# Attention in a hybrid encoder layer: scores and transposes take three PSUM banks in turn, the sums of two units alternate between two banks of their own

## The chip, the cores and the metric

The kernel runs on one core of a Trainium2 chip (trn2). The metric is device microseconds of one execution, lower is better. Engines are named as in the profile: PE is TensorE's matmul row and PEld its weight loads, DVE is VectorE, ACT is ScalarE, POOL is GpSimd, SP is SyncE, which issues most of the DMAs.

## The reference, cut to what matters

One encoder layer over two sequences of 1024 and 2048 tokens, each with 16 meta tokens ahead: an input projection, two branches (neighbourhood attention and mLSTM), a gated merge and an output projection. The change touches the attention branch alone:

```python
s_win = jnp.einsum('bcqhd,bwckhd->bhcqwk', q_blk, k_blk) * scale      # scores of a window
s_win = jnp.where(valid, s_win + bias, NEG)
s_met = jnp.einsum('bcqhd,bmhd->bhcqm', q_blk, km) * scale            # scores of the meta keys
p = jax.nn.softmax(jnp.concatenate([s_met, s_win], axis=-1), axis=-1)
out = einsum('bhcqm,bmhd->bcqhd', p_met, vm) + einsum('bhcqwk,bwckhd->bcqhd', p_win, v_blk)
```

## The kernel before

The kernel interleaves two streams of work on PE by hand: a "dense" one (projections, merge, output projection: the lines L218 to L220, L787 to L789, L988 to L990, L1953 to L1955) and a "sparse" one (mLSTM and attention). `run` (L2124) draws pieces of the dense stream between the steps of the sparse one, by cost numbers in microseconds that stand in the code. PE's order is therefore the order of the code. The order on DVE, ACT and the queues is chosen by a scheduler that simulates the program's timeline when it is built, so it can shift when a wait changes.

Attention is done per sequence, in two stages: `na(0, ...)` for the short one and `na(1, ...)` for the long one. A *unit* is one head, eight grid rows and one of four column blocks: 128 queries against 288 to 512 keys. The first stage has 64 units, the second 128. Unit u passes through these steps, which `na` (L1104) pipelines over four units, with dense work at each `yield`:

- step 1 of turn u: **scores** S(u), `na_scores` (L1230). Two matmuls (L1241, L1242) write a PSUM bank; then DVE adds the bias in place and takes the row's extremum (L1245).
- step 2 of turn u: **exponential** E(u), `na_exp` (L1251). ACT reads the bank and writes `prb` in SBUF (L1256). In the same step DVE scales unit u-1 (L1265, L1266).
- step 3 of turn u+2: **transposes** T(u), `na_turn` (L1268). Three or four transposes of `prb` (L1273) into a bank; ACT copies them to `pts` as the high part (L1275).
- step 4 of turn u+2: **low part** of the transposes, `na_low` (L1278). DVE reads the bank again (L1280).
- step 4 of turn u+3: **sums** O(u), `na_out` (L1282). Three or four matmuls (L1288) of the values with `pts`. Two units, an even and the following odd one, share a bank: half of 512 columns each.
- turn u+5 for an even u: the pair's sums are copied by ACT (`na_copy`, L1295) and added by two DVE instructions (`na_add`, L1302), which frees the bank.

PSUM has eight banks, given out by name (`psum`, L212) from `BANKS` (L41): three `pj` for the dense work, two `tr`, one `sc`, two `sm`.

```python
BANKS = dict(pj=3, tr=2, sc=1, sm=2)
```

A request for a name with several banks gets the one that was released longest ago, and the first matmul into it waits for whoever last read or wrote it. Before the change the scores of even units take `sc` and those of odd units `sm`; transposes take `tr`; the sums of a pair take `sm`. In the built program the scores of an odd unit u and the pair of sums that is opened in the same turn (units u-3 and u-2) stand one after the other in the same bank of `sm`, and the next odd turn uses the other one. So the first sum matmul of a pair, in step 4 of turn u, waits for E(u), which is issued in step 2 of that turn.

Of the kernel before, what the change touches and what calls it, by code (L numbers as in the profile page):

```python
# [3 lines left out]

# [1 line left out]

# [12 lines left out]
P = 128  # L19
# [56 lines left out]
def _row_types(R):  # L76

    out = []
    for t in range(R // 8):
        if t == 0:  # L80
            out.append((0, 0, 11))
        elif t == R // 8 - 1:
            out.append((2, R - 12, 12))
        else:
            out.append((1, 8 * t - 4, 15))
    return out
# [52 lines left out]
class K:  # L139
# [3 lines left out]
    def __init__(self, tc, ins, outs):  # L143
        self.tc, self.nc = tc, tc.nc
        self.xs = []
        self.i, self.o = ins, outs
        self.wreq, self.wraw, self.wrdy, self.wout = deque(), deque(), deque(), 0
        self.wseen, self.wkept, self.xkept = set(), {}, {}
        self.rwait = {}
        self.xput, self.turn, self.last, self.turns = deque(), 0, None, False  # L150
        self.marks, self.loose = {}, True
        self.need = False
        self.hold, self.early = deque(), True
        self.sides, self.qd, self.TD = [], {}, {}
# [949 lines left out]
    def na(self, s, rts):  # L1104

        tc, nc, i = self.tc, self.nc, self.i
        rows = _row_types(SEQLEN[s] // 64)
        with tc.tile_pool(name=f"na{s}{rts[0]}", bufs=1, side="right", reuse_waits="tile") as np_:
            self.qB = [np_.tile([P, 4, P], F32R, name=f"qB{j}") for j in range(2)]
            self.kx = [np_.tile([P, 16, 64], F32R, name=f"kx{j}") for j in range(2)]  # L1110
            self.gts = [np_.tile([P, 17, 48], F32, name=f"gt{j}") for j in range(2)]
            for q in self.qB:
                nc.gpsimd.dma_start(q[64:128], i["onehot"].rearrange("a (b c) -> a b c", b=4))
            for g in self.gts:
                nc.gpsimd.memset(g[:, 0, :], 0.0)
                nc.gpsimd.memset(g[:, 16, :], 0.0)
            heads = [(rt, pr, hh) for rt in rts for pr in range(4) for hh in range(2)]
            n = len(heads)
            prep = self.na_prep(np_, s, rows, heads, 0)
            self.na_bias(rows, heads, 0)  # L1120
            for k in range(6):
                next(prep, None)
                for _ in range(2 if k else 17 - 5 * s):
                    yield A_N[s]
            cur, nxt = self.head, None
            units = [(j, cb) for j in range(n) for cb in range(4)]
            ready = {}
            n_ = len(units)
            pairs = {}
            for u in range(n_ + 4):  # L1130
                if u >= 5 and u % 2:
                    self.na_copy(ready[u - 5], pairs[u - 5])
                    if u > n_:
                        self.na_add(ready[u - 5], pairs.pop(u - 5), s)
                if u < n_:
                    j, cb = units[u]
                    if cb == 0:
                        cur = self.head
                        prep = self.na_prep(np_, s, rows, heads, j + 1) if j + 1 < n else iter(())
                        next(prep, None)  # L1140
                    ready[u] = [cur, heads[j], cb, None, None, self.gts[j % 2], None]
                    self.na_scores(np_, ready[u], rows)
                    if j + 1 < n and cb == 0:
                        self.na_bias(rows, heads, j + 1)
                yield A_N[s]
                if u < n_:
                    self.na_exp(np_, ready[u])
                if 1 <= u <= n_:
                    self.na_scale(np_, ready[u - 1])
                if 5 <= u <= n_ and u % 2:  # L1150
                    self.na_add(ready[u - 5], pairs.pop(u - 5), s)
                if u < n_ and cb:
                    next(prep, None)
                if u == n_ + 3:
                    break
                yield A_N[s]
                if 2 <= u <= n_ + 1:
                    self.na_turn(np_, ready[u - 2])
                    if u < n_ and cb >= 2:
                        next(prep, None)  # L1160
                yield A_N[s]
                if 2 <= u <= n_ + 1:
                    self.na_low(ready[u - 2])
                if u >= 3:
                    if u % 2:
                        pairs[u - 3] = self.psum("sm", [P, 512])
                    self.na_out(ready[u - 3], pairs[(u - 3) // 2 * 2])
                yield A_N[s]
# [61 lines left out]
    def na_scores(self, np_, unit, rows):  # L1230
        nc = self.nc
        (stk, qb, kd, vt, yg, zt), (rt, pr, hh), cb = unit[:3]
        gt, c0 = unit[5], OFFC[cb] + 1
        typ, _, nr = rows[rt]
        ns = nr + 1
        kc, nb, g0 = KC0[cb], NKB[cb], (5, 1, 0)[typ]
        w, N = 8 * nb, 8 * nb * ns
        self.turns = not self.turns
        sc = self.psum("sc" if self.turns else "sm", [P, 512])
        so = sc[:, :N].rearrange("p (a b) -> p a b", b=w)  # L1240
        nc.tensor.matmul(so, stk[:, cb, :], kd[:, :ns, kc:kc + w], start=True, stop=False)  # L1241
        nc.tensor.matmul(so, qb[:, cb, :], self.kx[hh][:, :ns, kc:kc + w], start=False, stop=True)  # L1242
        pr_ = np_.tile([P, 512], F32, name="prb", bufs=3)
        mx = np_.tile([P, 1], F32, name="mx", bufs=4)
        nc.vector.tensor_tensor_reduce(  # L1245
            out=so, in0=so, in1=gt[:, g0:g0 + ns, c0:c0 + w],
            op0=ALU.add, op1=ALU.min, scale=-1.0, scalar=3.0e38, accum_out=mx)
        unit[3] = (pr_, mx, nb, 8 * ns)
        unit[6] = sc
# [18 lines left out]
    def na_turn(self, np_, unit):  # L1268
        nc = self.nc
        pr_, _, nb, ks = unit[3]  # L1270
        pt = self.psum("tr", [P, 4, P])
        for ch in range(nb):
            nc.tensor.transpose(pt[:ks, ch, :], pr_[:, ch * ks:(ch + 1) * ks], self.ident)  # L1273
        pts = np_.tile([P, 4, 2, P], F32R, name="pts", bufs=2)
        nc.scalar.activation(pts[:ks, :nb, 0, :], pt[:ks, :nb], AF.Copy)  # L1275
        unit[4], unit[6] = pts, pt
# [930 lines left out]
```

## Time and profile before

| | |
|---|---|
| time, median of 3 | 2664.87 us (2664.18 to 2667.11) |
| profiled execution, its own time | 2665.67 us |
| its span, first to last instruction | 2663.9 us |
| mean granted TensorE clock | 0.997 |
| first attention stage | about 815 to 1175 us of the span |
| second attention stage | about 1928 to 2556 us |
| last dense work behind it | 2556 to 2664 us |

A row of a view of groups has the source line, the engine, the operation, the tiles (written, then read), how many, the busy time, the mean of one, and the idle time of the engine just before them with what ended it. A row of the view of waits reads: engine, tile and line that waited, what it waited for; total, times, longest. A row of the timeline reads: start, duration, engine, line, operation, and in brackets the idle time of its engine before it with what ended it. Matmuls are pipelined and their ends are modelled: a PE row's duration is longer than the distance to the next row's start, so a short stall can hide under the row ahead of it.

### The profile page before, as it was taken

Reading aid. Unit: us, or ns where it says so; the run is one execution under the profiler, and the core shown is the slowest. Engines: PE = TensorE matmul, PEld = TensorE weight load, DVE = VectorE, ACT = ScalarE, POOL = GpSimd, SP = SyncE. Lnnn points to the kernel's source line nnn. Section 1 sums busy time; section 2 is a strip of 40 time slices with the busy share of each in tenths; the row PEclk is TensorE's granted clock in tenths of the full one; section 3 lists DMA queues with packets and bytes.
Section 4 is the critical chain, followed back from the end, with each engine's and each line's share of the span. In section 5 each row is a group of like instructions: output and inputs, shape, how many; then the busy total and the mean of one; then the engine's idle time right before and its main releaser. Section 6 shows DMA issues by size and latency. Waiting matters only on the chain.

```text
span 2663.9 us, 46683 instructions
## 1 busy us (share of the span) xinstructions
PE 2635.1 (99%) x15928; PEld 2328.5 (87%) x15928; DVE 1915.0 (72%) x5070; ACT 1423.7 (53%) x3292; POOL 196.3 (7%) x418
## 2 busy tenths in 40 slices
PE   9999999999999999999999999999999999999998
PEld 7898897899988999878888888878889898989888
DVE  5655678788776877546676776857478889797854
ACT  5423555555445554546665676656366655656521
POOL 0111131011301124000000000000000000000000
PEclk9999999999999999999999999999999999999999
DMA  9899988799866999978889998899899899898965
GB/s 371 328 332 337 332 302 303 279 339 344 313 218 242 352 324 309 317 230 268 261 269 342 370 295 260 282 348 324 275 323 321 283 306 286 284 306 266 326 244 206
DMA packets 393517, 800.47 MB, mean 300 GB/s; under 512 B 50528, under 2 KB 173360, under 8 KB 389440
## 3 DMA queue, kind: packets, MB, share of 16 engines
q1 hardware_dynamic: 361728, 697.24, 77.9%
q0 software_dynamic: 31552, 100.25, 10.2%
q8 instruction: 126, 2.06, 0.3%
q14 instruction: 111, 0.91, 0.1%
HBM read 543.72 MB, written 253.60 MB: 299 GB/s over the span
## 4 chain that ended last, share of the span: by engine, by line
PE 91%; DMA 4%; DVE 3%; ACT 1%; issue 1%; SPq 0%; DVEq 0%; ACTq 0%
PE pj L218 10%; PE pj L220 10%; PE pj L219 10%; PE pj L988 8%; PE pj L990 8%; PE pj L989 8%; PE pj L787 5%; PE pj L789 5%; PE pj L788 5%; PE pj L1954 3%; PE pj L1953 3%; PE pj L1955 3%; PE sm L1288 3%; PE tr L1273 2%; PE sm L220 1%; PE sm L219 1%
## 5 line engine op out<-in xcount | busy, mean ns | idle before, releaser
L218 PE MATMUL pj<-xh,whl 128*128 128x512 f32 (+1 forms) x960 | 369.7, 385 | 3.1 <-ACT xh L445 2.5
L220 PE MATMUL pj<-xh,whl 128*128 128x512 f32 (+1 forms) x960 | 361.0, 376 | 0.0
L219 PE MATMUL pj<-xl,whl 128*128 128x512 f32 (+1 forms) x960 | 360.3, 375 | 0.2 <-DVE xl L446 0.2
L787 PE MATMUL pj<-whl,xh 128*128 128x256 f32 (+1 forms) x1152 | 329.0, 286 | 0.0
L789 PE MATMUL pj<-whl,xl 128*128 128x256 f32 (+1 forms) x1152 | 325.3, 282 | 0.0
L788 PE MATMUL pj<-whl,xh 128*128 128x256 f32 (+1 forms) x1152 | 324.9, 282 | 0.0
L1953 PE MATMUL pj<-whl,mh 128*128 128x256 f32 x768 | 218.3, 284 | 1.1 <-DMA whl<-w 1.1
L787 PEld LDWEIGHTS pj<-whl,xh 128*128 128x128 f32 x1152 | 217.1, 188 | 0.4
L788 PEld LDWEIGHTS pj<-whl,xh 128*128 128x128 f32 x1152 | 217.0, 188 | 0.2
L789 PEld LDWEIGHTS pj<-whl,xl 128*128 128x128 f32 x1152 | 217.0, 188 | 0.0
L1954 PE MATMUL pj<-whl,mh 128*128 128x256 f32 x768 | 216.3, 282 | 0.0
L1955 PE MATMUL pj<-whl,mlo 128*128 128x256 f32 x768 | 215.5, 281 | 0.0
L218 PEld LDWEIGHTS pj<-xh,whl 128*128 128x128 f32 x960 | 181.2, 189 | 35.3 <-ACT xh L445 3.4
L220 PEld LDWEIGHTS pj<-xh,whl 128*128 128x128 f32 x960 | 181.2, 189 | 35.0
L219 PEld LDWEIGHTS pj<-xl,whl 128*128 128x128 f32 x960 | 181.8, 189 | 30.4 <-issue 1.0
L988 PE MATMUL pj<-xh,whl 128*128 128x512 f32 x512 | 206.7, 404 | 1.3 <-ACT pj L1005 1.1
L990 PE MATMUL pj<-xh,whl 128*128 128x512 f32 x512 | 202.0, 395 | 0.0
L989 PE MATMUL pj<-xl,whl 128*128 128x512 f32 x512 | 201.1, 393 | 0.0
L1280 DVE TENSOR_TENSOR pts<-tr,pts 96x384 fp32r<-96x384 f32 (+2 forms) x192 | 118.6, 618 | 63.8 <-ACT pts L1275 62.4
L1275 ACT ACTIVATE pts<-tr 96x384 fp32r<-96x384 f32 (+2 forms) x192 | 103.5, 539 | 101.7 <-PE tr L1273 101.1
L218 PE MATMUL pj<-yh,whl 128*128 128x512 f32 x384 | 154.1, 401 | 0.0
L219 PE MATMUL pj<-yl,whl 128*128 128x512 f32 x384 | 151.5, 395 | 0.7 <-DVE yl L1855 0.7
(380 smaller groups left out, 6824.9 us busy)
## 6 DMA issues: line engine op xcount, KB each, us to landing
whl<-w SPq DMA_DIRECT2D x131, 1024.0 KB
whl<-q SPq DMA_DIRECT2D x112, 512.0 KB
w<-whl SPq DMA_DIRECT2D x36, 1024.0 KB
wraw<-wu SPq DMA_DIRECT2D x48, 512.0 KB
gt<-st SPq DMA_DIRECT2D x96, 256.0 KB
tg<-gt SPq DMA_DIRECT2D x96, 256.0 KB
q<-po POOLq DMA_DIRECT2D x26, 512.0 KB, 7.3
xt<-xt SPq DMA_DIRECT2D x24, 512.0 KB
```

The source lines that it names most:

```text
L218: mm(out, ah, bh, start=start, stop=False)
L219: mm(out, ah, bl, start=False, stop=False)
L220: mm(out, al, bh, start=False, stop=stop)
L787: nc.tensor.matmul(o, xh, wh, start=k == 0, stop=False)
L788: nc.tensor.matmul(o, xh, wl, start=False, stop=False)
L789: nc.tensor.matmul(o, xl, wh, start=False, stop=k == KT - 1)
L988: mm(bank, w[:, 0, k], xh[:, k], start=fresh and k == 0, stop=False, skip_group_check=True)
L989: mm(bank, w[:, 0, k], xl[:, k], start=False, stop=False, skip_group_check=True)
L990: mm(bank, w[:, 1, k], xh[:, k], start=False, stop=k == 3, skip_group_check=True)
L1953: nc.tensor.matmul(o, mh[:, k, xs], wh, start=clear > 0 and k == 0, stop=False)
L1954: nc.tensor.matmul(o, mh[:, k, xs], wl, start=False, stop=False)
L1955: nc.tensor.matmul(o, ml[:, k, xs], wh, start=False, stop=clear < 2 and k == KT - 1)
```

## The change

It changes which bank each product is written to and nothing else: the same instructions on every engine, and PE's in the same order. A cycle over the names `sc`, `tr`, `tr` is made at the start of a stage; each request of `na_scores` and of `na_turn` takes its next name. Scores and transposes alternate on PE from the third unit on (S(u), T(u-2), S(u+1), T(u-1), ...), so each of the three banks is used again by the third request behind. The sums of the pairs are then the only users of `sm` in the stage and alternate between its two banks.

```diff
@@ na
+            self.banks = cycle(("sc", "tr", "tr"))
             heads = [(rt, pr, hh) for rt in rts for pr in range(4) for hh in range(2)]
@@ na_scores
-        self.turns = not self.turns
-        sc = self.psum("sc" if self.turns else "sm", [P, 512])
+        sc = self.psum(next(self.banks), [P, 512])
@@ na_turn
-        pt = self.psum("tr", [P, 4, P])
+        pt = self.psum(next(self.banks), [P, 512]).rearrange("p (a b) -> p a b", a=4)
```

The field `turns` and its start value in the constructor go, and `cycle` is imported.

PE in the second attention stage, transposes T(103) and the sums O(102) behind them, which open a pair in the turn of S(105); the names in brackets are the engines whose semaphores a row waits for. Before:

```order
L220 MATMUL pj<-yh,whl 128x512
L1273 MATMUL tr<-ident,prb 128x128 [waits DVE_49,PE_49]
L1273 MATMUL tr<-ident,prb 128x128 x2
L1288 MATMUL sm<-pts,vt 128x256 [waits Activation_49]
L1288 MATMUL sm<-pts,vt 128x256 x3
L218 MATMUL pj<-yh,whl 128x512 [waits DMAHW2_49]
```

And now:

```order
L220 MATMUL pj<-yh,whl 128x512
L1273 MATMUL sc<-ident,prb 128x128 [waits DVE_49,Activation_49]
L1273 MATMUL sc<-ident,prb 128x128 x2
L1288 MATMUL sm<-pts,vt 128x256 [waits DVE_49]
L1288 MATMUL sm<-pts,vt 128x256 x3
L218 MATMUL pj<-yh,whl 128x512 [waits DMAHW2_49]
```

The order is the same. The sums' wait for ACT is gone and one for DVE stands there (the low part of their own unit); the transposes, which waited for DVE and for PE's own earlier matmuls, now wait for ACT.

The first attention stage has the same order on all engines. In the second one the scheduler places some 70 of DVE's instructions and some 35 of ACT's a few rows earlier or later, and nine DMA issues of SP. DVE at 2148 to 2151 us of the profiled span, where the scaling of unit 110 (L1266, which T(110) needs) stands; L1226 splits the values of a head, L1918 and L1922 are the merge's. Before:

```order
L1265 RECIPROCAL sm<-sm 128x1 [waits Activation_49]
L1922 TENSOR_TENSOR mlo<-tg,mh 128x512 [waits Activation_49]
L1302 TENSOR_TENSOR yg<-sm,yg 64x2x8x16 [waits Activation_49]
L1266 TENSOR_SCALAR prb<-prb,sm 128x512 [waits DVE_49]
L1226 TENSOR_TENSOR vt<-vr,vt 128x8x64 [waits DMAHW6_49,DMAHW5_49,Activation_49]
L1918 SCALAR_TENSOR_TENSOR tg<-tg,pj 128x512 [waits DMAHW7_49,PE_49]
```

And now (the lines between 1117 and 1239 count one higher, so L1227 is L1226 of before):

```order
L1265 RECIPROCAL sm<-sm 128x1 [waits Activation_49]
L1302 TENSOR_TENSOR yg<-sm,yg 64x2x8x16 [waits Activation_49]
L1227 TENSOR_TENSOR vt<-vr,vt 128x8x64 [waits DMAHW6_49,DMAHW5_49,Activation_49]
L1918 SCALAR_TENSOR_TENSOR tg<-tg,pj 128x512 [waits DMAHW7_49,PE_49]
L1922 TENSOR_TENSOR mlo<-tg,mh 128x512 [waits Activation_49]
L1266 TENSOR_SCALAR prb<-prb,sm 128x512 [waits DVE_49]
```

The scaling of unit 110 now stands behind L1226 and L1918, which it stood ahead of.

More of the change, by code (lines that the diff above doesn't have):

```diff
@@ L2 @@
 from contextlib import ExitStack, contextmanager
-from itertools import chain
+from itertools import chain, cycle
 import numpy as np
@@ L149, in __init__ @@
         self.rwait = {}
-        self.xput, self.turn, self.last, self.turns = deque(), 0, None, False
+        self.xput, self.turn, self.last = deque(), 0, None
         self.marks, self.loose = {}, True
```

## The prediction

> **What bounds the kernel now.** I read the page's busy times and its chain of waits first, then the busy time by stage, then the waits of PE and PEld on the line of the sums, and last the timeline at single stalls. The page, on engines and on the chain that ended last:
>
> ```profile
> PE 2635.1 (99%) x15928; PEld 2328.5 (87%) x15928; DVE 1915.0 (72%) x5070; ACT 1423.7 (53%) x3292; POOL 196.3 (7%) x418
> ...
> PE 91%; DMA 4%; DVE 3%; ACT 1%; issue 1%; SPq 0%; DVEq 0%; ACTq 0%
> ```
>
> PE sets the end: 99% of the span, 91% of the chain. As PE's instructions and their order stay, only time in which PE stands still can be won, plus time that new stops would cost. By stretch (start:end, length, then busy time and count of PE, PEld, DVE, ACT, POOL, then granted clock, DMA share, GB/s), the second attention stage, the dense work behind it, and two pieces of the stage:
>
> ```profile
> 1928.00:2556.00 628.00, 625.52 (x4102) 567.35 (x4101) 526.89 (x1241) 372.23 (x855) 2.05 (x4) 1.00 0.92 296
> 2556.00:2664.00 108.00, 98.70 (x649) 89.87 (x647) 53.30 (x135) 15.62 (x51) 0.00 (x0) 0.98 0.65 235
> 2110.00:2124.00 14.00, 12.69 (x65) 10.37 (x64) 13.25 (x31) 5.36 (x12) 0.00 (x0) 1.00 0.99 348
> 2350.00:2386.00 36.00, 35.11 (x177) 28.76 (x176) 35.33 (x76) 19.05 (x39) 1.02 (x2) 1.00 0.99 315
> ```
>
> The stage's PE is shown idle for 628.00 - 625.52 = 2.5 us only, while DVE has 101 us to spare over the stage, but none in the two pieces (13.25 of 14 us, 35.33 of 36). What PE and its weight loads wait for at the sums (engine, line, releaser: total, times, longest; then the view of that line, with its second releaser), and the sums in the first stage's groups:
>
> ```profile
> PE sm L1288 <- ACT prb L1256: 2.2, 4, 1.3
> ...
> PEld sm L1288 <- ACT prb L1256: 5.5, 10, 1.5
> ...
>   ACT sqj L1959: 0.3, 1
> ...
> L1288 PE MATMUL sm<-pts,vt 96*128 96x256 f32 (+1 forms) x221 | 37.1, 284 | 0.0
> ```
>
> So the sums wait for an exponential in the same bank, PE by 2.2 us in four places, PEld by 5.5 + 0.3 = 5.8 us in eleven. In the first stage the line has no idle time: nothing is to be won there. The second stage opens 64 pairs so, and only eleven show a stop.
>
> **What is removed, and its size.** The two readings differ because a PE row's modelled end covers a short stop, and a load after a 512-wide matmul shows idle time even where PE does not stop. One place calibrates that:
>
> ```profile
> 2012.21 0.40 PE L220 MATMUL pj<-yh,whl 128*128 128x512 f32 x1
> 2012.44 0.50 PE L1288 MATMUL sm<-pts,vt 96*128 96x256 f32 x2
> ...
> 2012.44 0.41 PEld L1288 LDWEIGHTS sm<-pts,vt 96*128 96x128 f32 x3 [0.28 <-ACT prb L1256]
> ```
>
> Starts of PE are 0.23 us apart, the pace of a 512-wide matmul, so PE lost nothing, though the load shows 0.28 us. After a 512-wide matmul the load's reading is thus about 0.27 too high. The largest stop, and two more of the same kind, show both cases:
>
> ```profile
> 2117.90 0.40 PE L220 MATMUL pj<-yh,whl 128*128 128x512 f32 x1
> 2118.14 0.49 PE L1273 MATMUL tr<-ident,prb 128*128 128x128 f32 x3
> 2118.72 0.49 ACT L1275 ACTIVATE pts<-tr 128x384 fp32r<-128x384 f32 x1 [3.26 <-PE tr L1273]
> 2119.11 0.68 ACT L1256 ACTIVATE prb<-sm,mx 128x512 f32<-128x512 f32 x1
> 2119.93 0.38 PE L1288 MATMUL sm<-pts,vt 128*128 128x256 f32 x1 [1.31 <-ACT prb L1256]
> 2119.93 0.19 PEld L1288 LDWEIGHTS sm<-pts,vt 128*128 128x128 f32 x1 [1.55 <-ACT prb L1256]
> ...
> 2364.97 0.40 PE L220 MATMUL pj<-yh,whl 128*128 128x512 f32 x1
> 2365.64 0.50 PE L1288 MATMUL sm<-pts,vt 128*128 128x256 f32 x2 [0.26 <-ACT prb L1256]
> 2365.63 0.41 PEld L1288 LDWEIGHTS sm<-pts,vt 128*128 128x128 f32 x3 [0.70 <-ACT prb L1256]
> ...
> 2374.79 0.49 PE L1273 MATMUL tr<-ident,prb 128*128 128x128 f32 x3
> 2375.74 0.75 PE L1288 MATMUL sm<-pts,vt 128*128 128x256 f32 x4 [0.46 <-ACT prb L1256]
> ...
> 2385.59 0.42 PEld L1288 LDWEIGHTS sm<-pts,vt 128*128 128x128 f32 x3 [0.40 <-ACT prb L1256]
> ```
>
> At 2365.64 the true loss is 2365.64 - 2364.97 - 0.23 = 0.44, which is the load's 0.70 less 0.26. At 2119.93 three transposes stand ahead; they start 2118.14 and take about 0.25 us of PE, so the loss is 1.54, which is the load's 1.55 without correction. Five of the eleven loads follow a 512-wide matmul (2012.44, 2108.99, 2267.82, 2365.64, 2501.87). **Removed: 5.8 - 5 x 0.27 = 4.5 us**, between 2.2 (PE's reading) and 5.8 (PEld's). The exponential that the sums waited for was itself queued behind the copy of the transposes on ACT (2118.72 before 2119.11), so the old wait fell where DVE, and with it the row's extremum, ran late.
>
> A page speaks to the choice: the Trainium skill, Perfetto Trace Analysis, in Identifying the Most-Contended Engine, calls matmul busy time a bad measure, since matmuls are pipelined, and weight loads' busy time a good one. By that rule the sum would use 5.8, not 4.5. The row at 2012.44 here shows the load's reading to be too high as well, so the rule is followed by half.
>
> **What is added: three kinds of waits.** Scores and transposes now take a bank whose last user is the low part (L1280, DVE) or the exponential (L1256, ACT) of the third request behind; a pair of sums takes the bank that the pair two back left to L1302. Going through all requests of both stages with the times of before, the tightest of each kind are these: transposes after an exponential, scores after a low part, sums after an addition.
>
> ```profile
> 2135.96 0.58 ACT L1256 ACTIVATE prb<-sc,mx 128x384 f32<-128x384 f32 x1
> 2138.46 0.49 PE L1273 MATMUL tr<-ident,prb 128*128 128x128 f32 x3
> ...
> 2417.88 0.56 DVE L1280 TENSOR_TENSOR pts<-tr,pts 104x384 fp32r<-104x384 f32 x1
> 2420.87 0.31 PE L1241 MATMUL sm<-kd,stk 128*128 128x312 f32 x1
> ...
> 2504.30 0.40 DVE L1302 TENSOR_TENSOR yg<-sm,yg 64x256 f32<-64x256 f32 x1
> 2511.18 0.60 PE L1288 MATMUL sm<-pts,vt 104*128 104x256 f32 x3
> ```
>
> The margins are 2138.46 - 2136.54 = 1.92 us, 2420.87 - 2418.44 = 2.43 us, and 2511.18 - 2504.70 = 6.48 us. Most requests have more than twice the first. With the times of before none of the new waits stops PE: **0**, and up to the price in the third rival below if DVE or ACT slip by more than 1.9 us against PE. Behind a stopped transpose would queue all of PE's dense work, then DVE's merge that reads `pj`. The transposes' wait for PE's own matmuls goes; it cost nothing: L220 to the transposes is 2118.14 - 2117.90 = 0.24, the dense pace.
>
> **What comes back.** PE 4.5 us earlier meets the same DVE. The sums must still wait for the low part of their own unit, now their only wait. Its tightest place, right behind the full stretch:
>
> ```profile
> 2399.12 0.56 DVE L1280 TENSOR_TENSOR pts<-tr,pts 128x384 fp32r<-128x384 f32 x1
> 2400.30 0.48 PE L1288 MATMUL sm<-pts,vt 128*128 128x256 f32 x2
> ```
>
> The margin is 2400.30 - 2399.68 = 0.62 us. From 2365 to 2386 PE wins 0.44 + 0.70 + 0.40 = 1.54 us, and DVE, which is full there, wins nothing. If the low part keeps its time, 1.54 - 0.62 = 0.92 us is lost again; if DVE uses what PE hands it earlier, 0. I take **0.5**.
>
> The scheduler's new order has one place where a wait of PE loses margin, the scaling of unit 110, now behind L1226 and L1918:
>
> ```profile
> 2149.07 0.47 DVE L1266 TENSOR_SCALAR prb<-prb,sm 128x512 f32<-128x512 f32 x1
> 2149.46 0.67 DVE L1226 TENSOR_TENSOR vt<-vr,vt 128x512 fp32r<-128x512 f32 x1
> 2150.06 0.67 DVE L1918 SCALAR_TENSOR_TENSOR tg<-tg,pj 128x512 f32<-128x512 f32 x1
> ...
> 2153.45 0.60 PE L1273 MATMUL tr<-ident,prb 128*128 128x128 f32 x4
> ```
>
> It moves by about 0.6 + 0.6 = 1.2 us (distances of the starts), of a margin of 2153.45 - 2149.54 = 3.9 us, of which PE's earlier arrival takes 1.54 + 0.35 (the stops at 2119.93 and 2149.84) = 1.9. 0.8 us are left: **0**, at worst 0.6 if the merge's L1922 stands between as well. The other moved rows of DVE and ACT have neighbours of 0.4 to 0.7 us and margins of several: 0. The nine moved DMA issues on SP load weights and merge rows; what PE lost to late weights is
>
> ```profile
> PE pj L1953 <- DMA whl<-w: 1.1, 1, 1.1
> ...
> PE pj L218 <- DMA whl<-w: 0.5, 1, 0.5
> ```
>
> so the cover, weights loaded ahead of PE, holds nearly everywhere. Moved by a place they cost 0; if the cover fails once, another stop of 0.5 to 1.1.
>
> **Sum.** -4.5 + 0 + 0.5 + 0 = -4.0 us. The profiled execution took 2665.67 (span 2663.9), which gives 2661.7 (span 2659.9). It stands 0.8 above the median of the runs, 2664.87, so the median to expect is **2660.9**; with the bounds of the terms 2658.5 (5.8 and a little from a quicker DVE) to 2663 (2.2 and nothing but small losses).
>
> **Rivals.**
>
> *First: nothing gained.* DVE is full in 2110 to 2124 and 2350 to 2386, and most of the 4.5 us lies there (1.54 + 1.54). A PE that does not wait at the sums waits a few us later at the next thing DVE owes it, the low part of the sums' own unit or the scaling ahead of the transposes. For it: the two shares, and the 0.62 margin. Against it: that margin is the least one in the stage, most others exceed 2 us, more than any single gain, and DVE has 101 us to spare over the stage in which it recovers. 4.5 - 0.5 remains in my forecast; here all but about 1 us comes back: 2664.
>
> *Second: more.* The load's idle time is right and nothing comes back: 2664.87 - 5.8 = 2659.1. For it: the weight loads run ahead and a delayed one may cost more than the distance of starts shows. Against it: the calibration at 2012.44, and at 2501.87, where the load shows 0.29 and PE's starts are 0.25 apart.
>
> *Third: slower, by the three banks.* Before, a score took its bank four units or so behind and transposes had two banks of their own; now any low part or exponential that comes 1.9 us later than today stops PE at scores or transposes. It decides where DVE is full: 14 + 36 = 50 us, at 628 / 128 = 4.9 us a unit some 10 units, each with two requests. A stop of the size of those on the sums' line (5.5 / 10 = 0.55 us) at each of the 20 would cost 11 us: 2664.9 - 4.5 + 11 = 2671.4. Against it: not one of the margins is under 1.9 us in these very stretches, and PE arrives at most 1.5 us earlier there.
>
> *Fourth: slower, by the clock.* The stage's granted clock is 1.00, in the last 108 us 0.98. Were the stage to run at 0.98, 2% of 628 = 12.6 us less the 4 would give 2673.5. Against it: the clock is 1.00 with today's stops, and fewer follow. The Trainium skill, TensorE: Matmul & The Clock Gate, in A second HAM failure mode: psum-queue depth-cycling, tells of a kernel whose PE idled shortly between groups as it cycled PSUM banks and lost clock by it; the row of 1928 to 2556 does not bear that out here.
>
> That the change does not do what it says is excluded by the order: the wait for ACT is gone from the sums' row.
>
> **Chances.** Forecast 57%, nothing gained 18%, more 13%, three banks 8%, clock 4%. A measurement of this kernel tells about 0.2% from no change, that is 5.3 us: under 2659.5 is faster, over 2670.2 slower. Faster: the 13% and a quarter of the forecast's own range (2658.5 to 2663), together 27%. Slower: 12% less a part of the third rival that stops only a few times, 10%. Same: 63%. The range runs from 2657.5 to 2667, which holds the forecast, the first rival and the second and leaves out the last two and tails.
>
> **What would show it.** Right: the row of L1288 waiting for `prb` is gone from PE and PEld; PE's idle time in the stage falls by about 2 of the 2.5 us; the gaps at 2119.93, 2365.64, 2375.74 and 2385.59 close; the span is about 2660; a new wait of the sums for `pts` of L1280 near 2395, up to 0.9. Wrong: waits of PE at L1241 or L1273 for L1280, L1256 or L1266 of a microsecond in sum; or a new wait for weights; or a granted clock under 1.00 in the stage.

## The result, and the profile after

The changed kernel took 2661.70 us (median of 20 runs, 2659.54 to 2665.48) beside 2666.91 us for the kernel before in the same comparison. One of the 20 runs of the kernel before, at 3676.39 us, lies far outside the others (2662.91 to 2669.82) and is left out of the ratio. The ratio is 0.9984 with a 95% interval of 0.9977 to 0.9990: faster by 2.7 to 6.1 us. That is about the 0.2% (5.3 us) below which the prediction calls a kernel the same, so the class is "same", though the interval over all runs is clear of zero. The profiled execution took 2659.54 us, its span 2657.6.

The page after, on the same lines as before (engines, then the chain that ended last):

```profile
span 2657.6 us, 46668 instructions
...
PE 2630.8 (99%) x15928; PEld 2326.8 (88%) x15928; DVE 1911.1 (72%) x5070; ACT 1420.7 (53%) x3292; POOL 195.7 (7%) x418
...
PE 94%; DMA 3%; DVE 2%; ACT 1%; issue 0%; SPq 0%; DVEq 0%; ACTq 0%
```

PE's share of the chain rises from 91% to 94%. By stretch, the second attention stage and the two pieces where DVE is full:

```profile
1928.00:2556.00 628.00, 628.00 (x4149) 572.89 (x4148) 525.10 (x1242) 370.33 (x856) 2.04 (x4) 1.00 0.94 297
...
2110.00:2124.00 14.00, 14.00 (x73) 11.66 (x72) 13.81 (x30) 7.88 (x17) 0.00 (x0) 1.00 1.01 374
2350.00:2386.00 36.00, 36.00 (x189) 30.33 (x188) 35.46 (x78) 20.59 (x43) 1.02 (x2) 1.00 1.01 319
```

PE shows no idle time at all in the stage (628.00 of 628.00, before 625.52), though DVE is as full in the two pieces as before. The granted clock stays 1.00.

A total over the span mixes the change with stretches that it does not touch: the time from the last sums of the first stage to the first scores of the second differs between the profiles of this study, from 740.4 to 744.1 us. So I measure **each attention stage by itself**, from its first scores matmul to its last sums matmul. For the second stage, here are the first scores and the group of all sums, before and then after (the group's row has the least, median and most duration in ns, then the first and the last start in us):

```profile
1920.28 0.30 PE L1241 MATMUL sc<-kd,stk 128*128 128x288 f32 x1
...
L1288 PE MATMUL sm<-pts,vt x672: 277/282/386, 836.7 to 2554.4; 96*128 96x256 f32 x56, 104*128 104x256 f32 x56, 128*128 128x256 f32 x56
```

```profile
1919.18 0.30 PE L1241 MATMUL sc<-kd,stk 128*128 128x288 f32 x1
...
L1288 PE MATMUL sm<-pts,vt x672: 277/282/368, 838.0 to 2548.2; 96*128 96x256 f32 x56, 104*128 104x256 f32 x56, 128*128 128x256 f32 x56
```

With the starts in hundredths: 2554.39 - 1920.28 = 634.11 us before, 2548.18 - 1919.18 = 629.00 after. The second stage is **5.1 us shorter**. The first stage takes 356.86 and 356.85. The rest of the profile's 6.1 us, 1.0, lies outside both.

Where the 5.1 us went is seen by setting PE's rows of the two traces side by side, instruction by instruction. The distance between them grows within the stage only at the first sums of pairs, by 0.1 us or more at each of twelve places that stopped before (2012.44, 2108.99, 2119.93, 2149.84, 2247.38, 2267.82, 2365.64, 2375.74, 2385.59, 2424.66, 2472.66, 2501.87). The largest one, before and after:

```profile
2117.90 0.40 PE L220 MATMUL pj<-yh,whl 128*128 128x512 f32 x1
2118.14 0.49 PE L1273 MATMUL tr<-ident,prb 128*128 128x128 f32 x3
2119.93 0.74 PE L1288 MATMUL sm<-pts,vt 128*128 128x256 f32 x4 [1.31 <-ACT prb L1256]
2120.51 0.40 PE L218 MATMUL pj<-yh,whl 128*128 128x512 f32 x1
```

```profile
2116.62 0.49 PE L1273 MATMUL sc<-ident,prb 128*128 128x128 f32 x3
2116.86 0.72 PE L1288 MATMUL sm<-pts,vt 128*128 128x256 f32 x4
2117.42 0.39 PE L218 MATMUL pj<-yh,whl 128*128 128x512 f32 x1
```

From the transposes to the matmul behind the sums it was 2.37 us, now 0.80: 1.57 us won, as the same work now runs at PE's own pace.

### The profile page after: what moved, and what is told of

Read it like the earlier page. It is cut to its first block, busy times and chain, and to the rows that moved or that the text cites. A ratio compares the mean times of both kernels' runs of the same rounds, so it can differ in the third digit from the quotient of the medians.

```text
span 2657.6 us, 46668 instructions
## 1 busy us (share of the span) xinstructions
PE 2630.8 (99%) x15928; PEld 2326.8 (88%) x15928; DVE 1911.1 (72%) x5070; ACT 1420.7 (53%) x3292; POOL 195.7 (7%) x418
## 4 chain that ended last, share of the span: by engine, by line
PE 94%; DMA 3%; DVE 2%; ACT 1%; issue 0%; SPq 0%; DVEq 0%; ACTq 0%
PE pj L218 10%; PE pj L220 10%; PE pj L219 10%; PE pj L988 8%; PE pj L990 7%; PE pj L989 7%; PE pj L787 5%; PE pj L789 5%; PE pj L788 5%; PE pj L1954 3%; PE pj L1953 3%; PE pj L1955 3%; PE sm L1288 3%; PE tr L1273 2%; PE sc L1273 1%; PE tr L1241 1%
## 5 line engine op out<-in xcount | busy, mean ns | idle before, releaser
L218 PE MATMUL pj<-xh,whl 128*128 128x512 f32 (+1 forms) x960 | 369.5, 385 | 3.8 <-ACT xh L445 2.0
L220 PE MATMUL pj<-xh,whl 128*128 128x512 f32 (+1 forms) x960 | 360.9, 376 | 0.0
L218 PEld LDWEIGHTS pj<-xh,whl 128*128 128x128 f32 x960 | 180.9, 188 | 36.2 <-ACT xh L445 2.8
L220 PEld LDWEIGHTS pj<-xh,whl 128*128 128x128 f32 x960 | 181.2, 189 | 35.0
L218 PE MATMUL pj<-yh,whl 128*128 128x512 f32 x384 | 154.1, 401 | 0.0
L220 PE MATMUL pj<-yh,whl 128*128 128x512 f32 x384 | 152.1, 396 | 0.0
L1953 PEld LDWEIGHTS pj<-whl,mh 128*128 128x128 f32 x768 | 144.7, 188 | 2.0 <-DMA whl<-w 1.2
```

The costliest lines, as they stand in the source:

```text
L218: mm(out, ah, bh, start=start, stop=False)
L220: mm(out, al, bh, start=False, stop=stop)
L1953: nc.tensor.matmul(o, mh[:, k, xs], wh, start=clear > 0 and k == 0, stop=False)
```

## The experiments

All times of stages below are read as above, from one profile each. A profile's second stage is repeatable to some 0.6 us (stages with equal order: 634.11 and 634.72; 629.00 and 629.38), the whole execution only to some 6 us (2659.54 to 2665.48 over the change's runs), so the stages decide and the ratios over all runs stand beside them.

**Which stage brings it.** In the kernels named stage2_only and stage1_only the new cycle is used in one stage, the banks of before in the other (`s` is 0 in the first stage; the cut shows stage2_only, stage1_only has the two choices exchanged):

```diff
-            self.banks = cycle(("sc", "tr", "tr"))
+            self.banks, self.tb = (cycle(("sc", "tr", "tr")),) * 2 if s else (cycle(("sc", "sm")), cycle(("tr",)))
@@ na_turn
-        pt = self.psum(next(self.banks), [P, 512])...
+        pt = self.psum(next(self.tb), [P, 512])...
```

> The second attention stage has the new banks, the first one those of before. Theory (the gain is the stops of the second stage's sums behind an exponential in the same bank): the whole gain, 4 to 5.5 us under the kernel before, PE starts in the first stage as before, no idle of PE at the sums. Rival (part of the gain comes from the first stage, whose new banks might move DVE or ACT ahead): clearly less, 1 to 3 us under.

> The first attention stage has the new banks, the second one those of before. Theory: 0 +- 1 us against the kernel before, and the stops at the sums of the second stage are all there (about 5.5 us of weight-load idle behind the exponential). Rival: a gain of 2 us or more.

| | first stage | second stage | ratio to before (95%) |
|---|---|---|---|
| before | 356.86 | 634.11 | |
| the change | 356.85 | 629.00 | 0.9984 (0.9977 to 0.9990) |
| second stage only | 356.86 | 629.38 | 0.9983 (0.9974 to 0.9993) |
| first stage only | 356.85 | 634.72 | 0.9996 (0.9988 to 1.0005) |

All of it comes from the second stage. With the first stage alone the old wait is there in full (its view of waits):

```profile
PEld sm L1288 <- ACT prb L1256: 6.0, 11, 1.5
```

The second-stage kernel shows the one wait that the prediction named as what comes back, the sums' own low part, at the place that it named (2400.30 of before):

```profile
2392.98 0.56 DVE L1280 TENSOR_TENSOR pts<-tr,pts 128x384 fp32r<-128x384 f32 x1
2392.98 0.49 PE L1273 MATMUL sc<-ident,prb 128*104 128x128 f32 x3
2393.59 0.42 PEld L1288 LDWEIGHTS sm<-pts,vt 128*128 128x128 f32 x3 [0.37 <-DVE pts L1280]
```

In the change's own profile the same low part starts at 2393.89 and the sums at 2394.63, with 0.18 us to spare. The two programs have the same order of DVE and ACT in this stage; an execution decides whether 0 or 0.4 us come back there.

**Is it the sums' own banks, or the rotation?** sums_alone gives the sums their two banks as the change does, but no rotation: transposes keep `tr`, all scores take `sc`. two_banks keeps the rotation and shortens it: scores and transposes share only `tr`, `tr`, and `sc` lies idle in attention. (The cut shows the cycles alone; in sums_alone `na_turn` draws from `self.tb` as above.)

```diff
-            self.banks = cycle(("sc", "tr", "tr"))
+            self.banks, self.tb = cycle(("sc",)), cycle(("tr",))     # sums_alone
+            self.banks = cycle(("tr",))                              # two_banks
```

> The sums of the pairs alternate between their two banks as in the change, transposes keep their pair as before, and all scores take the one bank sc. Theory (only the sharing of the sums' bank counted, margins decide the rest): the stops at the sums go (-4.9 us by the starts of PE in the second stage), and a score now waits for the exponential of the unit just before it; with the times of the changed kernel this is late in six places of the second stage by 3.0 us together, the worst at 2143 us by 1.7 and at 2240 by 0.5; net about 2 us under the kernel before (0.5 to 4). Rival (the three banks in rotation bring the gain): nothing gained or slower. Second rival (a late score delays the exponential, the scaling and the transposes behind it, and DVE does not catch up): 5 us or more above the changed kernel.

> Scores and transposes rotate over two banks (tr, tr) instead of three; sc lies idle in both attention stages; sums as in the change. Theory: margins shrink from 1.5 us at least to late in eleven places of the second stage, by 2.6 us together with the times of the changed kernel, 0 in the first stage; about 2.5 us above the changed kernel, 1 to 4 us under the kernel before. Rival (a stop in a rotation that is too short repeats through the whole stretch where DVE is full, about 20 requests at 0.55 us): 10 us or more above the changed kernel, so slower than before.

| | first stage | second stage | ratio to before (95%) |
|---|---|---|---|
| sums_alone | 356.85 | 632.78 | 0.9990 (0.9981 to 0.9999) |
| two_banks | 356.85 | 629.87 | 0.9977 (0.9968 to 0.9986) |

sums_alone went by the theory: the stops at the sums are gone, and new ones stand at scores behind the exponential of the unit before, 1.84 us at 2142.92 of the change's trace, 0.70 at 2240.27, 0.5 and 0.4 at 2415 and 2421. It keeps 1.3 of the 5.1 us, where about 2 was expected. Its view of waits, and the worst stop:

```profile
PE sc L1241 <- ACT prb L1256: 2.6, 4, 1.7
...
2142.62 0.69 ACT L1256 ACTIVATE prb<-sc,mx 128x512 f32<-128x512 f32 x1
2143.46 0.44 PE L1241 MATMUL sc<-kd,stk 128*128 128x384 f32 x1 [1.66 <-ACT prb L1256]
```

two_banks missed: 0.9 us longer than the change, not 2.5, with only one stop that PE shows:

```profile
PE tr L1273 <- DVE pts L1280: 0.5, 1, 0.5
```

This stop, at 1997.19, makes 0.62 of the 0.9 us between the two traces: the transposes wait until a low part has left their bank, and DVE had stood 1.18 us for a transfer ahead of that low part.

The expectation had laid the two banks, in strict turn, over the times of the change's trace. In strict turn the largest stop would be that of sums_alone, at the score that starts there at 2142.92, 1.7 us before the exponential of the unit before ends. No such stop came, because in two_banks this score did not take that exponential's bank. It took the bank of the transposes ahead of it, which their low part had just left, and it starts while the exponential is still to come:

```profile
2144.44 0.55 DVE L1280 TENSOR_TENSOR pts<-tr,pts 128x384 fp32r<-128x384 f32 x1
2145.20 0.33 PE L1241 MATMUL tr<-kd,stk 128*128 128x384 f32 x1
2146.19 0.69 ACT L1256 ACTIVATE prb<-tr,mx 128x512 f32<-128x512 f32 x1
```

So the two banks are not used in strict turn. Next in size, the transposes near 2413 came 0.6 us ahead of the low part that they would wait for. That low part was late through a transfer: DVE's L1211 ahead of it waits for ACT's L1209, and this for the queries of the next head, which landed 3.96 us after ACT was ready in the one execution and 2.96 us in the other (start, duration, engine, line; the change first, two_banks second):

```profile
2411.78 0.63 ACT L1209 ACTIVATE qB<-stk 64x512 fp32r<-64x512 f32 x1 [3.96 <-DMA stk<-nq]
```

```profile
2413.21 0.63 ACT L1209 ACTIVATE qB<-stk 64x512 fp32r<-64x512 f32 x1 [2.96 <-DMA stk<-nq]
```

So margins read from one trace hold to about 1 us where a transfer stands behind them, and the scheduler also placed some twenty rows of DVE otherwise. What follows: at the present load the sums' own banks are what counts; a third bank in the rotation is worth 0.9 us at most, and that is hardly more than one profile differs from the next. Two banks' ratio over all runs is not above the change's.

**Where does it turn round?** The third rival of the prediction, and the first, hang on DVE. Two idle multiplications of a scratch tile of 128x240 behind each scaling (0.278 us each by their rows) were put into three kernels (the cut leaves out the making of the tile):

```diff
@@ na_scale
         nc.vector.tensor_scalar(pr_[:, :N], pr_[:, :N], sm, None, op0=ALU.mult)
+        nc.vector.tensor_scalar(self.junk, self.junk, 1.0, None, op0=ALU.mult)
+        nc.vector.tensor_scalar(self.junk, self.junk, 1.0, None, op0=ALU.mult)
```

> The kernel before, with two idle multiplications of a 128x240 scratch tile behind each scaling: some 0.3 us each by the scaling's rows of the same kind, 2 x 128 x 0.3 = 77 us of DVE in the second stage, which had about 101 to spare; 2 x 64 x 0.3 = 38 in the first, which has 111 to spare. The result is not touched. Theory: the extrema and so the exponentials come later, and many more of the 64 pairs stop at their first sum: the second stage 10 to 30 us longer than before's 634.1. The first stage stays within 2 us of 356.9.

> The changed kernel with the same extra DVE work. Theory (the margins of the three banks, 1.5 us at the least and over 4 at the median, take up most of it): the second stage grows less than in the kernel before with the same load, 2 to 15 us over 629.0; the gap between the two second stages widens from 5.1 us to 8 to 20. Rival (a three-bank rotation ties PE to DVE at two requests a unit, so a late DVE stops it more often than the sums did before): the gap shrinks below 5.1 or turns round.

> Two banks in rotation for scores and transposes, sums as in the change, with the same extra DVE work. Theory: margins of 2 us at the median against over 4 are used up, so its second stage is 5 to 25 us longer than that of the three banks with the same load, though without the load it was only 0.9 longer. Rival (the third bank is not needed even under load; all that matters is that the sums have their own banks): within 2 us of it.

| with scratch work | first stage | second stage | ratio to before (95%) |
|---|---|---|---|
| before | 357.42 | 639.44 | 1.0016 (1.0007 to 1.0026) |
| the change | 357.18 | 632.62 | 0.9992 (0.9981 to 1.0002) |
| two banks | 357.14 | 633.61 | 0.9999 (0.9989 to 1.0008) |

The load did not fall as intended: nothing depends on the scratch tile, so the scheduler placed all of it ahead: in the change's trace its last rows start at 2177, before the longer of the two full pieces. For the first 250 us of the stage the test stands, with a gap of 6.8 us in place of 5.1, under the 8 to 20 expected. The other two expectations failed as well: the kernel before grew by 5.3 us, not by 10 to 30, and two banks stand 1.0 us over three, not 5 to 25 (their rival had said within 2). The weight loads' waits at the sums (L1292 here), before and after with the load:

```profile
PEld sm L1292 <- ACT prb L1258: 10.6, 14, 2.2
PEld sm L1292 <- DVE pts L1284: 1.0, 1, 1.0
```

```profile
PEld sm L1292 <- DVE pts L1284: 1.0, 1, 1.0
```

To hold the load to its unit, the second set multiplies the first 240 columns of the scaled tile itself by 1.0, once or twice. The work stands in the chain from the exponential to the transposes:

```diff
@@ na_scale
         nc.vector.tensor_scalar(pr_[:, :N], pr_[:, :N], sm, None, op0=ALU.mult)
+        nc.vector.tensor_scalar(pr_[:, :240], pr_[:, :240], 1.0, None, op0=ALU.mult)
+        nc.vector.tensor_scalar(pr_[:, :240], pr_[:, :240], 1.0, None, op0=ALU.mult)
```

> The kernel before; each scaling is followed by two multiplications of the first 240 columns of its own tile by 1.0 (0.278 us each by the scratch rows of the run with scratch work), so that the load falls evenly on the 128 units of the second stage and cannot be done ahead: 71 us of DVE. The product stays the same. Where DVE is full already (36 + 14 us, some ten units) it is short of about 4 to 5 us, whatever the banks. Theory: second stage 645 to 660, as that deficit and more stops at the sums behind exponentials come together.

> The changed kernel with the same load in the chain. Theory: the deficit of 4 to 5 us is paid at the sums' own low part, at the transposes and at the scores, the stops behind exponentials are not: second stage 633 to 645, at least 7 us shorter than the kernel before with this load. Rival (a late DVE now stops PE at two requests a unit): gap under 5.1 us or turned round.

> Two banks for scores and transposes, with the same load in the chain. If the third bank's margin matters under load: 5 us or more above the three banks with this load. If it is the sums' own banks that matter and the third bank is spare: within 2 us, as without the load (0.9) and with the scratch work (1.0).

> The kernel before with one multiplication by 1.0 in the chain in place of two: 36 us of DVE in the second stage. Theory: between 634.1 without load and 647.7 with two; the stops at the sums (12 at present) become more, and DVE is short of 2 to 2.5 us in the full stretches: 637 to 642.

> The changed kernel with one multiplication by 1.0 in the chain. Theory (the gain is what DVE's slack lets PE keep; it is 5.1 us without load and -1.7 with two): 635 to 641, 1 to 4 us under the kernel before with this load. Rival (the loss of the gain came from the length of single stops and the clock that fell to 0.50 after them, and one multiplication makes no stop over 3 us): the whole 5 us or more.

| second stage | no load | once (36 us of DVE) | twice (71 us) |
|---|---|---|---|
| before | 634.11 | 639.05 | 647.67 |
| the change | 629.00 | 638.24 | 649.37 |
| two banks | 629.87 | | 646.29 |
| gain of the change | 5.1 | 0.8 | -1.7 |
| first stage, before / change / two banks | 356.86 / 356.85 / 356.85 | 356.85 / 356.85 / - | 356.97 / 357.21 / 360.39 |
| ratios to the kernel before, before / change | 1 / 0.9984 | 1.0009 / 1.0003 | 1.0054 / 1.0050 |

With once, the change keeps 0.8 us, hardly more than profiles of one order differ (1 to 4 were expected). With twice, the theory's 7 us or more failed and nothing is left. Two banks are 3.1 us shorter than three in the second stage and 3.2 us longer in the first, which fits neither of their two expectations. Over all runs the kernels with twice are the same within their intervals (1.0037 to 1.0071, 1.0035 to 1.0065, 1.0036 to 1.0066). PE's waits in the two kernels with twice, before and then the change:

```profile
PE tr L1275 <- DVE prb L1268: 9.3, 5, 3.2
...
PE sm L1290 <- ACT prb L1256: 2.5, 2, 1.2
```

```profile
PE sc L1275 <- DVE prb L1268: 6.7, 3, 3.6
...
PE tr L1275 <- DVE prb L1268: 5.0, 5, 2.2
...
PE tr L1275 <- DVE sm L1265: 2.0, 2, 1.7
```

The waits of the change in the second stage are for the scaling (`prb` of its multiplications, `sm` of the reciprocal), not for a bank: the data are late, and no choice of banks helps. The request that comes closest to the last user of its bank there is the transposes at 2271.55, still 0.73 us behind the end of that exponential. Before, the sums' wait took a part of the same lateness; without it the transposes take nearly all (9.3 + 2.5 = 11.8 us and 6.7 + 5.0 + 2.0 = 13.7). So with three banks the third rival's mechanism, a rotation that binds, was not seen even here; the first rival's, DVE's lateness collected at the next wait, was.

With two banks the rotation does bind under load: scores and transposes wait for low parts (L1284, L1282) and scores for exponentials (L1256). Two banks with scratch work, and then with twice:

```profile
PE tr L1243 <- DVE pts L1284: 1.1, 1, 1.1
...
PE tr L1277 <- DVE pts L1284: 1.0, 1, 1.0
```

```profile
PE tr L1241 <- ACT prb L1256: 1.7, 2, 1.3
...
PE tr L1275 <- DVE pts L1282: 1.3, 2, 0.9
```

With twice, 2.6 us of these 3.0 stand in the first attention stage, at 905.26, 942.09 and 953.77. There neither the change nor the kernel before, with the same load, stops at scores or transposes, and this stage is the one that took 360.39 us in place of 357.21. So the third bank is spare at the present load, but not under every load. This is one profile of each kernel, and ACT had waited 4.16 us for a transfer ahead of the stop at 905.26.

A second cost goes with the longer stops: at some of them the granted clock falls. The stretches with a lower clock (start:end, and the clock behind POOL's column), in the kernel before with twice, in the change with twice, in the change with once:

```profile
2258.00:2262.00 4.00, 3.82 (x14) 3.33 (x15) 3.15 (x10) 0.60 (x1) 0.00 (x0) 0.57 1.12 305
```

```profile
2254.00:2262.00 8.00, 7.97 (x27) 6.73 (x28) 5.20 (x15) 0.98 (x2) 0.00 (x0) 0.63 1.12 305
2372.00:2378.00 6.00, 6.00 (x23) 5.01 (x22) 5.36 (x14) 0.60 (x2) 0.00 (x0) 0.72 1.10 276
```

```profile
2505.00:2511.00 6.00, 5.60 (x22) 4.92 (x23) 4.07 (x13) 2.28 (x6) 0.00 (x0) 0.72 1.04 374
```

By (1 - clock) x length they cost 4 x 0.43 = 1.7, 8 x 0.37 + 6 x 0.28 = 4.6, and 6 x 0.28 = 1.7 us; the kernel before with once has none. Two banks with twice have two such stretches, 2137 to 2143 and 2372 to 2378, at 0.72 each: 3.4 us. Without them the change would gain 0.8 + 1.7 = 2.5 us with once and -1.7 + 4.6 - 1.7 = 1.2 with twice, two banks with twice 1.4 + 3.4 - 1.7 = 3.1 in the second stage: a gain that shrinks with DVE's slack, as the theory of the last pair had it, and the clock on top of it. This split is an estimate from one profile of each kernel; no run took the clock out.

## Why the prediction was right, point by point

- **The bound.** PE sets the end, and the gain is stops of PE in the second stage alone: shown by the stages measured apart and by the two kernels with the change in one stage.
- **What is removed.** The mechanism was right, and so were all eleven places (a twelfth, at 2472.66, was not seen); the size was not. The sum took 4.5 us, by taking 0.27 off the load's idle reading in each of five places behind a 512-wide matmul. The measured 5.1 lies between that and the load's full reading of 5.8. The step that failed is the calibration at 2012.44: it looked at the start of the first sums matmul only. From L220 to the L218 behind the sums it took 2012.90 - 2012.21 = 0.69 us before, 2011.70 - 2011.11 = 0.59 now:

```profile
2012.21 0.40 PE L220 MATMUL pj<-yh,whl 128*128 128x512 f32 x1
2012.44 0.62 PE L1288 MATMUL sm<-pts,vt 96*128 96x256 f32 x3
2012.90 0.40 PE L218 MATMUL pj<-yh,whl 128*128 128x512 f32 x1
```

```profile
2011.11 0.39 PE L220 MATMUL pj<-yh,whl 128*128 128x512 f32 x1
2011.34 0.53 PE L1288 MATMUL sm<-pts,vt 96*128 96x256 f32 x3
2011.70 0.39 PE L218 MATMUL pj<-yh,whl 128*128 128x512 f32 x1
```

  The late load cost 0.10 us behind the first matmul, in the second one. The load's reading is then too high by 0.28 - 0.10 = 0.18. The other four such places bear this out: between the two traces they lost 0.32, 0.32, 0.52 and 0.10 us, where the loads read 0.50, 0.49, 0.70 and 0.29. The sum becomes 5.8 - 5 x 0.18 = 4.9. The rest, 0.2, is the stop at 2472.66 (0.13 by the starts) and roundings. The Trainium skill (Perfetto Trace Analysis, Identifying the Most-Contended Engine) prefers the busy share of weight loads to that of matmuls, as a measure of a whole kernel. For these stops the order agrees: the loads' 5.8 misses the measured 5.1 by 0.7, PE's 2.2 by 2.9. The corrected 4.5 misses it by 0.6, so the correction went the right way, and too far.
- **New waits at 0.** Right: no wait of PE at scores, transposes or the sums' add in the change's profile.
- **What comes back, 0.5.** It was 0 in the change's profile and 0.4 in that of stage2_only, in the predicted place. In the change's profile the sums there start 5.67 us earlier (2400.30 to 2394.63, 1.10 of it the stage's earlier start) and the low part 5.23 (2399.12 to 2393.89): all but 0.44 us, so most of DVE's queue moved with PE.
- **The scaling of unit 110, and the moved DMAs, at 0.** Nothing of either shows: the distance between the traces does not change there.
- **The rivals.** "Nothing gained" is false for this kernel and nearly true for the same kernel with 36 to 71 us more of DVE in the stage. "Slower by three banks" did not occur, with any load tried: the 1.7 us more with twice come from waits for data and from the clock. Nor did a lower clock (1.00 in the stage), which in the loaded kernels came only with stops longer than any in this stage.
- **The sum.** -4.0 was forecast; the stage measured -5.1, as the stops were 0.6 larger and the 0.5 did not come back; the runs measured -2.7 to -6.1. That the median, 2661.70, came within 0.8 us of the forecast 2660.9 is partly luck. The forecast started from a median of 3 runs, 2664.87, which is 2.0 us under the 2666.91 of 20, and its gain was 1.2 us less than the 5.2 between the two medians; the two errors cancel in part. The range, 2657.5 to 2667, held the first two rivals as well, so the time alone does not tell them from the forecast; the stages and the waits do.

What stays open: whether the 0.9 us between two_banks and the change would come again (one profile each, 0.62 of it at one stop), and the 1.0 us by which the rest of the change's profile is shorter. The clock may have a part in the latter: ahead of the second stage it reads 0.83 in 1190 to 1200 us and 0.77 in 1795 to 1810 in the profile before, 1.00 and 0.89 in the one after, and no run here ties that to the change. It is also open why two banks with twice are 3.1 us shorter than three in the second stage: 1.2 of it is the estimate for the clock, the rest has no run of its own.

## What to carry to other kernels

When buffers are given out by "longest free first", two users with different rhythms can fall into one buffer in lockstep, and an operation then waits for one that it has nothing to do with; give the user with the slack a buffer of its own and check with the trace's ends that the new partner is always early. Price a stop from the last undisturbed start ahead of it to the first start behind it, across the whole group, not by an idle column. Average spare time on a helper engine (here 101 of 628 us on DVE) says little of how much more it can take: 36 us more, inside the chain, ate 4.3 of the 5.1 us, some 1.7 of them through the clock. A buffer that looks spare at one load need not be spare at another: the third bank was worth under a microsecond here, and 3.2 us in the first stage with twice, which is 36 us of DVE work there.

## What the runs showed of the hardware that was not expected

A long stop can cost more than its length. In the kernel before with twice, PE stood still from L220 at 2254.62 to the transposes at 2258.18; the 512-wide matmuls behind ran 0.43 us apart in place of 0.23 for about 3 us, and then at full pace again, at a clock of 1.00 from 2262:

```profile
2254.62 0.40 PE L220 MATMUL pj<-yh,whl 128*128 128x512 f32 x1
2258.18 1.08 PE L1275 MATMUL tr<-ident,prb 128*128 128x128 f32 x4 [3.17 <-DVE prb L1268]
...
2259.92 0.63 PE L220 MATMUL pj<-yh,whl 128*128 128x512 f32 x1
2260.34 0.63 PE L218 MATMUL pj<-yh,whl 128*128 128x512 f32 x1
...
2262.23 0.39 PE L219 MATMUL pj<-yl,whl 128*128 128x512 f32 x1
```

The same came with the change's stops of 3.57 and 2.25 us with twice and of 1.93 us with once, and with two banks' of 2.80 and 2.23 with twice (PE's idle column). At the stop of 3.57 us the clock fell before PE went on: it reads 0.52 in 2253 to 2254, and the transposes start at 2254.03. Other stops of about 2 us had no such mark (the sums of the kernel before with once at 2291.91, 1.99 us), and neither had any in this stage of the kernel before itself, the longest of them 1.31. The Trainium skill, TensorE: Matmul & The Clock Gate, in Why this matters for your kernels, advises against idle gaps of PE above about 3 us between bursts; the two longest stops, 3.17 and 3.57, agree, and the four of 1.93 to 2.80 show that a smaller one can do it too. What tells those from the stop of 1.99 us without a mark, no run here shows.
